# An eight-column scratch result moved into a shared tile, and every later buffer 32 bytes lower

## The chip, the cores and the metric

One Trainium2 chip, one of its cores. The metric is the device time of one execution in microseconds (us): the median of 3 runs of the kernel before is 413.98 us (413.92 to 414.71).

## The reference

A trunk of two decoder layers over 256 tokens of width 1024, all in float32. Layer 0 normalises its input, multiplies it by one wide matrix (z, x, B, C, dt, q, k, v, g side by side), runs a Mamba-2 state-space mixer and a dilated window attention on the results, and multiplies both, side by side, by an output matrix. Layer 1 normalises, multiplies by q, k, v and gate matrices, runs causal attention, gates it, and multiplies by its output matrix. Cut to what matters here:

```
h = rms_norm(x, norm_w)
z, xbc, dt, q, k, v, g = split(h @ even_w_in)
mixed = concat([ssd(xbc, dt) gated by z, dilated_attention(q, k, v) gated by g])
x = x + mixed @ even_w_out
h = rms_norm(x, odd_norm_w)
q, k, v, g = split(h @ odd_w_in)
x = x + (moba_attention(q, k, v) * silu(g)) @ odd_w_out
```

Nearly all the arithmetic is in the products with the four weight matrices.

## The kernel before

**The products.** The weights lie in DRAM cut into tiles of 128 partitions by 2048 columns. `load_split` brings a tile into a buffer `raw` (three buffers, two DMA pieces each) and splits it into a part rounded to float32r, `whi` (a cast on ScalarE), and the rest, `wlo` (a subtraction on VectorE), three buffers of each. Activations are split in the same way: into `xh` and `xl`, one tile each with 8 blocks of 256 tokens, or into pairs of `mix` tiles (24 tiles of 256 columns). A product of float32 numbers is then three TensorE products, high by high, high by low, low by high. There are two forms of it:
- `proj_tok` and `out_proj` (through `mm3`): tokens come out on the partitions. The activations are the stationary operand (128 columns), a row of weights the moving one, 512 columns wide; in the last part of `out_proj`, some are 256 wide. The activations are `mix` tiles in the first three steps and in `out_proj`, and `xh`, `xl` elsewhere.
- `proj_fm`: features come out on the partitions. The weights are the stationary operand, `xh` or `xl` the moving one, 256 columns wide.

In the names of the profile `acc<-whi,xh` is a matmul into the tile acc with whi moving and xh stationary. The smaller products of the mixers and the transposes (`x<-cst,k`, `x<-cst,p` and so on) are plain float32.

**The order.** The program is recorded operation by operation, and the class `Plan` then orders it: it goes through simulated time with a price for every operation, gives an engine the first operation in order of recording that can start, and hands out the buffers of a tag (a set of equal tiles, as the 15 tiles `k2` of 512 columns) by the time of their release, the earliest first. All operations are emitted on one line, L519, in that order.

**The tile of the change.** Line 1252 in `trunk_kernel` issues the first activation of ScalarE, so that the function table is loaded while the first data are still on their way. Its result is never read. It goes to a tile `junk` of 8 columns, which has a tag of its own.

**Where the tiles lie.** Tiles are laid one behind another along the partition when their tag is first used, each rounded up to 32 bytes; the small constants come first. So in the program of the kernel before these start at the following bytes of a partition: xh 16512, xl 24704, cst 32896, all1 39520, k2 42688 (15 tiles of 2048 bytes), junk 73408 (32 bytes), mix 73440 (24 tiles of 1024), raw 98016, whi 122592, wlo 147168 (three tiles of 8192 each), qkT 173472 (four of 4096), p 192288 (18 of 1536), and small ones before, between and behind. xh, xl, cst and k2 start at multiples of 64; mix, raw, whi, wlo, qkT and p at 32 past a multiple of 64, and so does each tile of theirs.

Of the kernel before, what the change touches and what calls it, by code (L numbers as in the profile page):

```python
# [13 lines left out]
AF = mybir.ActivationFunctionType  # L14
# [7 lines left out]
P = 128  # L22
# [538 lines left out]
def trunk_kernel(ctx: ExitStack, tc: tile.TileContext, x, tiles_host, dtw_host, norms, xt_host, params, bparams, consts, causal_mask, out):  # L561
# [5 lines left out]
    pe, act, dve, gps, sp = plan.pe, plan.act, plan.dve, plan.pool, plan.sp  # L567
    count = [0]

    def sb(shape, dt=F32, tag=None, bufs=1, name=None):  # L570
        count[0] += 1
        return plan.tile(shape, tag or f"{name}_{count[0]}", bufs, dt=dt)

    def k2():
        return sb([P, 512], tag="k2", bufs=NK2)
# [53 lines left out]
    nhalf = sb([P, 8], name="nhalf")  # L629
# [619 lines left out]
        pe.matmul(wp[:, 0:128], warm[:, 0:128], warm[:, 0:128], start=True, stop=True)  # L1249
    dve.memset(all1, 1.0)  # L1250

    act.activation(sb([P, 8], name="junk"), nhalf, AF.Copy, scale=1.0)
    sp.dma_start(ncol, norms)
    xf = [two(k2()) for _ in range(4)]
    entry = [tuple(sb([P, S], F32R, tag="mix", bufs=24) for _ in range(2)) for _ in range(KD)]
# [78 lines left out]
    scale = k2()[:, :S]  # L1334
# [80 lines left out]
```

## Time and profile before

| | |
|---|---|
| median of 3 runs | 413.98 us (413.92 to 414.71) |
| the profiled execution | 413.3 us |
| its span, first to last instruction | 411.5 us |
| TensorE busy | 404.1 us |
| VectorE busy | 319.9 us |
| ScalarE busy | 259.5 us |
| read from DRAM | 67.28 MB |

Busy times come from one profiled execution. A busy TensorE is not a TensorE at its peak: consecutive matmuls overlap in the records, so their pace is read from the distance of their starts. The chain of work that ended last is followed back from the last instruction, at each step to what released it. PE is TensorE, PEld its weight loads, DVE VectorE, ACT ScalarE, POOL GpSimd, SP the engine that issues the DMAs.

### The profile page before, as it was taken

The numbers are of one execution on the slowest core, as the hardware profiler recorded it, in microseconds if no ns is written. First come the engines' busy times: TensorE is split into PE (matmuls) and PEld (weight loads), VectorE is DVE, ScalarE is ACT, GpSimd is POOL, SyncE is SP. The second block draws the span as 40 slices with busy tenths as digits, with TensorE's granted clock in tenths as the row PEclk, the third lists the DMA queues.
The fourth block names the chain that finished last, engine by engine and source line by source line (L and its number), as shares of the span: only waits on it lengthen the run. The fifth ranks groups of instructions, "written<-read, shape, count | busy, mean of one in ns | idle before, by whom it ended". The sixth has DMA issues, their size and how long they took to land.

```text
span 411.5 us, 7072 instructions
## 1 busy us (share of the span) xinstructions
PE 404.1 (98%) x2537; PEld 341.7 (83%) x2537; DVE 319.9 (78%) x810; ACT 259.5 (63%) x532; POOL 58.5 (14%) x65
## 2 busy tenths in 40 slices
PE   7999999999999999999999999999999999999996
PEld 6788999999888777778889888878878878879786
DVE  3888899998769999999929774697579856679622
ACT  5887655555346686567775945686559656667610
POOL 0160400000031100242004000013330004500000
PEclk9999999999999999999999999999999999999999
DMA  6995755357454426653645290546650834442003
GB/s 237 377 406 201 249 199 171 103 200 245 166 162 147 147 62 226 224 164 115 220 155 192 64 281 25 143 168 200 206 189 17 255 111 151 166 139 102 2 2 102
DMA packets 23139, 68.84 MB, mean 167 GB/s; under 512 B 4179, under 2 KB 5952, under 8 KB 23104
## 3 DMA queue, kind: packets, MB, share of 16 engines
q1 hardware_dynamic: 23104, 68.39, 49.7%
q8 instruction: 20, 0.33, 0.3%
q14 instruction: 15, 0.12, 0.1%
HBM read 67.28 MB, written 1.10 MB: 166 GB/s over the span
## 4 chain that ended last, share of the span: by engine, by line
PE 91%; DVE 4%; DMA 2%; POOL 1%; issue 1%; ACT 1%; SPq 1%; DVEq 0%
PE acc L519 71%; PE x L519 19%; DMA raw<-in_tiles_dram 2%; DVE wlo L519 1%; DVE k L519 1%; POOL rq L519 1%; DVE xl L519 1%; SPq L519 1%; DVE rq L519 0%; ACT xh L519 0%; ACT whi L519 0%; ACT k L519 0%; DVE t L519 0%; DVEq L519 0%
## 5 line engine op out<-in xcount | busy, mean ns | idle before, releaser
L519 DVE TENSOR_TENSOR wlo<-raw,whi 128x1024 fp32r<-128x1024 f32 (+1 forms) x117 | 140.2, 1212 | 17.5 <-ACT whi L519 17.2
L519 ACT CAST whi<-raw 128x1024 fp32r<-128x1024 f32 (+1 forms) x117 | 119.6, 1043 | 31.7 <-PE acc L519 22.1
L519 PE MATMUL acc<-xh,wlo 128*128 128x256 f32 x288 | 81.2, 282 | 0.0
L519 PE MATMUL acc<-xl,whi 128*128 128x256 f32 x288 | 81.1, 282 | 0.0
L519 PE MATMUL acc<-xh,whi 128*128 128x256 f32 x288 | 80.9, 281 | 0.0
L519 PE MATMUL acc<-whi,xh 128*128 128x512 f32 x192 | 77.8, 406 | 0.0
L519 PE MATMUL acc<-wlo,xh 128*128 128x512 f32 x192 | 77.6, 404 | 0.0
L519 PE MATMUL acc<-whi,xl 128*128 128x512 f32 x192 | 77.4, 403 | 0.0
L519 PE MATMUL acc<-whi,mix 128*128 128x512 f32 x216 | 70.6, 398 | 0.8 <-ACT whi L519 0.8
L519 PEld LDWEIGHTS acc<-xl,whi 128*128 128x128 f32 x288 | 54.3, 188 | 0.4 <-issue 0.2
L519 PEld LDWEIGHTS acc<-xh,whi 128*128 128x128 f32 x288 | 54.3, 189 | 0.2
L519 PEld LDWEIGHTS acc<-xh,wlo 128*128 128x128 f32 x288 | 54.3, 189 | 0.2 <-issue 0.2
L519 PEld LDWEIGHTS acc<-whi,mix 128*128 128x128 f32 x216 | 40.4, 188 | 9.9 <-ACT whi L519 1.8
L519 PEld LDWEIGHTS acc<-whi,xl 128*128 128x128 f32 x192 | 36.4, 189 | 8.9 <-issue 1.2
L519 PE MATMUL acc<-wlo,mix 128*128 128x512 f32 x108 | 43.1, 399 | 0.5 <-DVE wlo L519 0.5
L519 PEld LDWEIGHTS acc<-wlo,xh 128*128 128x128 f32 x192 | 36.4, 190 | 8.5 <-issue 1.4
L519 PEld LDWEIGHTS acc<-whi,xh 128*128 128x128 f32 x192 | 36.4, 189 | 8.1 <-issue 1.0
L519 POOL TENSOR_TENSOR rq<-rq,nhalf 128x8 f32<-128x8 f32 x20 | 36.6, 1831 | 1.5
L519 ACT COPY k<-acc 128x512 f32<-128x512 f32 x24 | 14.1, 586 | 25.3 <-PE acc L519 25.3
L519 PEld LDWEIGHTS acc<-wlo,mix 128*128 128x128 f32 x108 | 20.3, 188 | 5.7 <-DVE wlo L519 1.8
L519 ACT ACTIVATE k<-k 128x512 f32<-128x512 f32 x20 | 12.7, 638 | 18.4 <-DVE k L519 18.4
L519 DVE TENSOR_REDUCE rq<-k 128x8 f32<-128x512 f32 x20 | 13.6, 682 | 12.6 <-ACT k L519 12.6
(151 smaller groups left out, 554.6 us busy)
## 6 DMA issues: line engine op xcount, KB each, us to landing
raw<-in_tiles_dram SPq DMA_DIRECT2D x115, 512.0 KB, 4.8
k<-in_x_dram SPq DMA_DIRECT2D x8, 256.0 KB, 5.6
qkT<-cd SPq DMA_DIRECT2D x4, 512.0 KB, 3.7
k<-in_xt_dram SPq DMA_DIRECT2D x4, 256.0 KB, 6.0
out_dram<-k SPq DMA_DIRECT2D x8, 128.0 KB, 1.8
cst<-in_consts_dram SPq DMA_DIRECT2D x1, 640.0 KB, 9.6
raw<-in_tiles_dram SPq DMA_DIRECT2D x2, 256.0 KB, 4.7
cst<-in_causal_mask_dram SPq DMA_DIRECT2D x1, 192.0 KB, 2.3
```

The costliest lines, as they stand in the source:

```text
L519: getattr(eng[op.engine], op.method)(*[real(a) for a in op.args], **{k: real(v) for k, v in op.kw.items()})
```

## The change

The activation that brings the function table in gets the first 8 columns of a `k2` tile as its output, in place of the tile `junk`.

```diff
-    act.activation(sb([P, 8], name="junk"), nhalf, AF.Copy, scale=1.0)
+    act.activation(k2()[:, :8], nhalf, AF.Copy, scale=1.0)
```

The tag `junk` is gone and with it its 32 bytes. The tags first used after this line (mix, raw, whi, wlo, qkT, p and the small tiles among them) start 32 bytes lower; those first used before it (xh, xl, cst, all1, k2 and others) stay. One `k2` tile more is handed out, after the one that the warm-up uses.

## Rows read from the trace of the kernel before

**Rows 1.** The page: busy time, granted clock, chain that ended last by engine.
```profile
PE 404.1 (98%) x2537; PEld 341.7 (83%) x2537; DVE 319.9 (78%) x810; ACT 259.5 (63%) x532; POOL 58.5 (14%) x65
...
PEclk9999999999999999999999999999999999999999
...
PE 91%; DVE 4%; DMA 2%; POOL 1%; issue 1%; ACT 1%; SPq 1%; DVEq 0%
```

**Rows 2.** The chain in order of time: start us, us, what; five long pieces.
```profile
235 pieces in order of time: start us, us, what
...
18.00 14.12 PE acc L519 x62
...
76.53 27.34 PE acc L519 x233
...
343.43 15.87 PE acc L519 x68
...
397.27 8.19 PE acc L519 x36
...
405.46 2.88 PE x L519 x24
```

**Rows 3.** Groups by shape, PE, 18 to 32 us: busy us, mean ns | idle.
```profile
L519 PE MATMUL acc<-whi,mix 128*128 128x512 f32 x41 | 12.7, 390 | 0.0
...
L519 PE MATMUL acc<-wlo,mix 128*128 128x512 f32 x21 | 8.3, 393 | 0.0
```

**Rows 4.** The same view, 90 to 103 us: one of three alike forms.
```profile
L519 PE MATMUL acc<-xl,whi 128*128 128x256 f32 x38 | 10.6, 280 | 0.0
```

**Rows 5.** The same view, 344 to 358 us: one of three alike forms.
```profile
L519 PE MATMUL acc<-wlo,xh 128*128 128x512 f32 x21 | 8.4, 399 | 0.0
```

**Rows 6.** The same view, 405.5 to 408.3 us.
```profile
L519 PE MATMUL x<-whi,mix 128*128 128x256 f32 x16 | 3.0, 283 | 0.0
```

**Rows 7.** Timeline of ScalarE, 0 to 5 us: start us, us, what, count.
```profile
0.72 1.28 ACT L519 ACT_TABLE_LOAD   x1 [0.72 <-PEq L1386]
2.01 0.21 ACT L519 ACTIVATE junk<-nhalf 128x8 f32<-128x8 f32 x1
3.87 0.91 ACT L519 ACTIVATE mix<-k,ncol 128x256 fp32r<-128x256 f32 x2 [1.65 <-DMA k<-in_xt_dram]
```

**Rows 8.** Groups by shape, whole span: the same work at both places.
```profile
L519 PE MATMUL x<-cst,p 128*128 128x128 f32 x120 | 18.5, 275 | 0.0
...
L519 PE MATMUL x<-cst,k 128*128 128x128 f32 x96 | 14.5, 273 | 1.5 <-DVE k L519 1.5
...
L519 DVE TENSOR_TENSOR xl<-k,xh 128x512 fp32r<-128x512 f32 x4 | 2.7, 684 | 0.0
...
L519 DVE TENSOR_TENSOR wlo<-raw,whi 128x512 fp32r<-128x512 f32 x2 | 1.4, 692 | 2.1 <-ACT whi L519 2.1
...
L519 ACT CAST xh<-k 128x512 fp32r<-128x512 f32 x4 | 2.5, 616 | 0.0
...
L519 ACT CAST whi<-raw 128x512 fp32r<-128x512 f32 x2 | 1.2, 618 | 2.0 <-DMA raw<-in_tiles_dram 2.0
```

**Rows 9.** DMA issues: count, KB each, median us to landing.
```profile
k<-in_xt_dram SPq DMA_DIRECT2D x4, 256.0 KB, 6.0
...
raw<-in_tiles_dram SPq DMA_DIRECT2D x2, 256.0 KB, 4.7
```

**Rows 10.** Groups by shape, whole span: the large matmuls, for their counts.
```profile
L519 PE MATMUL acc<-xh,wlo 128*128 128x256 f32 x288 | 81.2, 282 | 0.0
...
L519 PE MATMUL acc<-whi,xh 128*128 128x512 f32 x192 | 77.8, 406 | 0.0
...
L519 PE MATMUL acc<-whi,mix 128*128 128x512 f32 x216 | 70.6, 398 | 0.8 <-ACT whi L519 0.8
...
L519 PE MATMUL acc<-wlo,mix 128*128 128x512 f32 x108 | 43.1, 399 | 0.5 <-DVE wlo L519 0.5
...
L519 PE MATMUL x<-whi,mix 128*128 128x512 f32 x24 | 7.9, 399 | 0.0
...
L519 PE MATMUL x<-whi,mix 128*128 128x256 f32 x32 | 6.1, 283 | 0.0
```

**Rows 11.** Busy time by stretch: PE, PEld, DVE, ACT, POOL, then clock, DMA share.
```profile
60.00:75.00 15.00, 15.00 (x127) 14.90 (x126) 15.00 (x31) 9.31 (x14) 0.00 (x0) 1.00 0.55 179
135.00:180.00 45.00, 45.00 (x238) 33.36 (x237) 44.53 (x119) 31.83 (x74) 6.74 (x8) 1.00 0.54 173
```

## The prediction

> **What bounds the kernel now.** I read the page first: TensorE is busy for 404.1 of 411.5 us and holds 91% of the chain that ended last [rows 1]. A change is therefore worth what it does to TensorE's pace, or to the few places where TensorE waits. Next I read the chain piece by piece, 235 pieces in all. A long piece of one kind, divided by its number of matmuls, is the distance from one matmul's start to the next; the "mean ns of one" in the group views is no such distance, because matmuls overlap there. The pieces give [rows 2]: 14.12 / 62 = 227.7 ns, 27.34 / 233 = 117.3 ns, 15.87 / 68 = 233.4 ns, 8.19 / 36 = 227.5 ns and 2.88 / 24 = 120.0 ns. What the stretches hold comes from the grouped views of windows inside them. 18 to 32 us is 512 columns wide, weights moving, the stationary operand in mix [rows 3]. 90 to 103 us has 256 columns, xh or xl moving, whi or wlo stationary [rows 4]. 344 to 358 us has 512 columns, weights moving, xh or xl stationary [rows 5]. The tail from 405.5 us has 256 columns, weights moving, mix stationary [rows 6].
>
> At the granted clock, full in nearly the whole span [rows 1], that is 2.4 GHz, 512 columns take 213.3 ns and 256 take 106.7 ns. So each matmul pays an extra 14.3, 20.1, 10.7 or 13.3 ns. The reader should see that 227.7 and 233.4 ns belong to the same operation with the same moving operand; only the place of the stationary tile differs. It is not the stage either: mix has 227.7 ns in the first steps, under full DMA load, and 227.5 ns near the end, where almost nothing else runs.
>
> **Where the bytes lie.** By the placement told above, before the change xh and xl start at a multiple of 64 bytes, and raw, mix, whi, wlo, qkT and p all start 32 bytes past one. After it the latter are at multiples of 64 too. Sorted in this way the rows read:
> - moving at 32, stationary at 32: extra 14.3 (512 columns) and 13.3 ns (256)
> - moving at 32, stationary at 0: extra 20.1 ns (512)
> - moving at 0, stationary at 32: extra 10.7 ns (256)
> - moving at 0, stationary at 0: the trace of before has none; this is what all of them become.
>
> 64 bytes are 16 columns, which is 6.67 ns at this clock. The extras are about 2, 3 and 1.6 such steps. The reading I take: one step always; one more when the moving operand begins in the middle of a 64-byte line and so touches one line more; and up to one more (1 at 512 columns, 0.6 at 256) when the two operands lie at different halves of a line and their reads get in each other's way. By that, both at 0 pay one step: 220.0 ns for 512 columns and 113.3 for 256. This is an estimate extended from four rows to a fifth case.
>
> **The change part by part.** (1) The instruction itself: an 8-column activation of 0.21 us on ScalarE at 2.01 us; ScalarE's next instruction starts only at 3.87 us, when a load has landed [rows 7]. It writes eight columns to another address: 0 us, covered by that wait of 1.65 us. (2) The free tile is one of the 15 k2 tiles. The planner hands tiles out by the earliest release, and this one is back before any other; only five tiles (the warm-up's and four loads) are taken before the first product's results, so no step has to wait for it and the planned order stays. The tile that inherits its place is written by ScalarE itself, which is in order: 0 us. Queues, DMAs and counts of instructions are otherwise the same.
>
> (3) 32 bytes for ScalarE and VectorE. The trace has the same operation at both places: a 512-column cast takes 618 ns from raw to whi (at 32) and 616 ns from k to xh (at 0); the 512-column subtraction takes 692 against 684 ns [rows 8]. For the 117 casts and subtractions this bounds the effect at 0 to -1 us of VectorE's busy time, off the path. TensorE's fp32 transposes from k (at 0) and p (at 32) have means of 273 and 275 ns [rows 8]; these I leave at 0.
>
> (4) DMA. A 256 KB transfer lands in 4.7 us in raw (at 32) and in 6.0 us in k (at 0) [rows 9]; nothing shows raw to be the slower, and DMA is 2% of the chain [rows 1]. I take 0, with bounds of -0.3 and +0.3 us for the start, where the chain hangs on loads.
>
> (5) TensorE's products, the one term that counts. The counts [rows 10]: 192 for each of three forms with xh or xl stationary, 576 in all; 216 + 108 + 24 with mix stationary and 512 columns, and half of 24 again for wlo, 360; 32 and half of it again, 48, with 256 columns; 288 for each of three forms with xh or xl moving, 864. So:
> - 576 x (233.4 - 220.0) = 7.7 us
> - 360 x (227.6 - 220.0) = 2.7 us
> - 48 x (120.0 - 113.3) = 0.3 us
> - 864 x (117.3 - 113.3) = 3.5 us
>
> Sum 14.2 us, if TensorE stays the bound everywhere. It does not quite. In 60 to 75 us VectorE is busy for all 15 us and in 135 to 180 us for 44.53 of 45 [rows 11], so there a faster TensorE waits for VectorE next. These 60 us are 15% of TensorE's time: 2.1 us of the sum less the 0.5 us that VectorE has free, 1.6 us lost. Most of the 235 pieces of the chain are short, with small products or waits between the large matmuls [rows 2]; as an allowance for these I take off a tenth of the remaining 12.6 us, 1.3 us. That leaves about 11 us. The span goes from 411.5 to 400.5 us; the profiled execution took 413.3 us, that is 1.8 us around the span, and comes to 402.3 us; the median of 413.98 is 0.7 above it, so I predict 403.0 us.
>
> The missing case is bounded from both sides by the nearest rows: no better than one step (the lowest extra, 10.7 ns, is between one and two), and no worse than the 20.1 ns of the only rows with a stationary tile at 0.
>
> **Rivals.** *Only part of it goes.* If the two effects hang on larger blocks than 64 bytes (xh begins at a multiple of 128, whi after the change does not), one of them stays. Taking away only the split line gives 936 x 6.67 + 48 x 6.67 = 6.6 us; taking away only the conflict gives 576 x 5.8 = 3.3 us, and 864 matmuls that end between 113.3 and 120.0, from -3.5 to +2.3 us. These give 407 to 413 us.
>
> *Slower: a stationary tile at a multiple of 64 is itself the bad case.* The one clean comparison in the trace, 233.4 against 227.6 ns, can be read so: +5.8 ns for every load of a tile at 0. Then the 864 matmuls with whi or wlo stationary, and the 408 with mix, all get it: 1272 x 5.8 = 7.4 us, all on the path, since a slower TensorE needs no cover; a moving operand at 0 may give back 936 x 2.7 = 2.5 us (120.0 against 117.3). About 419 to 421 us. It decides as soon as the stretch with mix stationary rises above 229 ns. For it: it needs no second effect. Against it: a tile at 0 fills fewer lines than one at 32.
>
> *No change.* xh and xl lie low in the memory, from byte 16512 to 32896, and mix far above, so the 5.8 ns can belong to the region, which 32 bytes don't alter; or the buffers do not move. Then 414.0 us. [...]
>
> **How the numbers follow.** Forecast as summed, 400 to 405 us: 0.40. Part of it, 405 to 413.1: 0.22. No change, 414.0 within 0.2%: 0.20. Slower by the rival, around 420: 0.18. A difference of 0.2%, 0.8 us, is about what measurements of this kernel can tell from none. Faster is therefore 0.62, same 0.20, slower 0.18. The range from 400.0 to 415.0 us takes in the first three and leaves the last out.
>
> **What would show it.** In the trace after: the long pieces of the chain at about 220 ns (512 columns, whether mix or xh is stationary), the 256-column stretch at about 113 ns, and VectorE nearer to full between 135 and 180 us of the old time. If xh falls to 227 and mix stays, the conflict alone is gone; if both fall by 6.7 and keep their distance, the split line alone. If mix rises to 233, the slower rival is right. If all four distances stay within 1 ns, addresses of this kind do not matter here, and the forecast is wrong at its root. If the distances fall as told and the time falls by under 7 us, the cover by VectorE was underestimated.

## The result, and the profile after

| | before | after |
|---|---|---|
| median | 413.95 us (413.54 to 414.71, 4 runs) | 409.01 us (408.95 to 409.77, 4 runs) |
| the profiled execution | 413.3 us | 408.95 us |
| its span | 411.5 us | 407.1 us |
| TensorE busy | 404.1 us | 399.1 us |

The ratio is 0.9883, with a 95% interval of 0.9864 to 0.9901: faster by 4.9 us or 1.2%. Faster was forecast, and 409.01 us lies in the range. But 11 us had been told, and the forecast as summed was 400 to 405 us: the range holds the time only because it takes in two of the rivals.

The page after, its lines of busy time and of the chain's engines, answers to [rows 1]:

```profile
PE 399.1 (98%) x2537; PEld 338.1 (83%) x2537; DVE 319.6 (78%) x810; ACT 259.5 (64%) x532; POOL 59.6 (15%) x65
...
PE 90%; DVE 4%; DMA 2%; POOL 1%; issue 1%; ACT 1%; SPq 1%; DVEq 0%
```

TensorE has 5.0 us less of products and 3.6 us less of weight loads. VectorE and ScalarE stayed within 0.3 us; GpSimd, 1% of the chain, has 1.1 us more. The chain in order of time (start us, us, what) shows where; these are the pieces of [rows 2]:

```profile
18.48 14.13 PE acc L519 x62
...
76.43 26.43 PE acc L519 x233
...
339.90 15.59 PE acc L519 x68
...
392.92 8.19 PE acc L519 x36
...
401.11 2.88 PE x L519 x24
```

The long pieces are the same, in the same order, so nothing here speaks for another planned order. By the counts: with mix stationary 14.13 / 62 = 227.9 ns and 8.19 / 36 = 227.5 ns, where 227.7 and 227.5 had been; in the tail 2.88 / 24 = 120.0 ns, as before. With xh stationary 15.59 / 68 = 229.3 ns, where 233.4 had been. With xh moving 26.43 / 233 = 113.4 ns, where 117.3 had been. The starts add it up: 0.5 us later than before at the first piece, 0.1 us earlier at the second, 3.5 us earlier at the third, 4.4 us earlier at the fourth.

The time from each start to the next, put down to the first of the two and summed over the whole trace, went from 105.8 to 102.6 us for the products with xh or xl moving, from 141.5 to 139.9 us for those with xh or xl stationary, and stayed at 88.1 and 5.6 us for those with mix. Unrounded that is 3.2 and 1.5, together 4.7 us; the small products took 0.3 us more, and so it accounts for the span's 4.4 us.

### The profile page after: what moved, and what is told of

Its sections match the earlier page's. It is cut to its first block, busy times and chain, and to the rows that moved or that the text cites. A ratio compares the mean times of both kernels' runs of the same rounds, so it can differ in the third digit from the quotient of the medians.

```text
span 407.1 us, 7072 instructions
## 1 busy us (share of the span) xinstructions
PE 399.1 (98%) x2537; PEld 338.1 (83%) x2537; DVE 319.6 (78%) x810; ACT 259.5 (64%) x532; POOL 59.6 (15%) x65
## 4 chain that ended last, share of the span: by engine, by line
PE 90%; DVE 4%; DMA 2%; POOL 1%; issue 1%; ACT 1%; SPq 1%; DVEq 0%
PE acc L519 71%; PE x L519 20%; DMA raw<-in_tiles_dram 2%; DVE wlo L519 1%; DVE k L519 1%; POOL rq L519 1%; DVE xl L519 1%; SPq L519 1%; DVE rq L519 0%; ACT xh L519 0%; ACT whi L519 0%; ACT k L519 0%; DVE t L519 0%; DVEq L519 0%
## 5 line engine op out<-in xcount | busy, mean ns | idle before, releaser
L519 PE MATMUL acc<-xh,wlo 128*128 128x256 f32 x288 | 80.2, 278 | 0.0
L519 PE MATMUL acc<-xl,whi 128*128 128x256 f32 x288 | 80.0, 278 | 0.0
L519 PE MATMUL acc<-xh,whi 128*128 128x256 f32 x288 | 79.9, 277 | 0.0
```

The costliest lines, as they stand in the source:

```text
L519: getattr(eng[op.engine], op.method)(*[real(a) for a in op.args], **{k: real(v) for k, v in op.kw.items()})
```

## The experiments

In what follows the distance is the moving operand's first byte less the stationary one's, modulo 256 (that 256 is the right number comes out of the map below). The time from one matmul's start to the next is called the pace. By the placement of the kernel before, weights start at 224 and xh at 128 modulo 256. So where xh is stationary the distance was 96, and where it moves 160. After the change (weights at 192) they are 64 and 192. Between weights and mix it is 0 both times.

**Is it the place, or the shared tile?** Two kernels separate them. The first keeps the shared tile and puts the 32 bytes back, as an edit of the changed kernel:

```diff
     act.activation(k2()[:, :8], nhalf, AF.Copy, scale=1.0)
+    pool.tile([P, 8], F32, name="pad")
```

> The changed kernel with an unused 32-byte tile behind the k2 tiles: the shared tile stays in use, all addresses are those of before. If the places of the buffers are the whole cause: the time of before, 413.9 us, with 117.3 and 233.4 ns in the two stretches. If the use of the shared tile (another order of buffers) is the cause: 409.0 us.

Measured: 413.89 us, 0.9994 of the kernel before (0.9979 to 1.0009). The second keeps the tile of its own, as an edit of the kernel before:

```diff
-    act.activation(sb([P, 8], name="junk"), nhalf, AF.Copy, scale=1.0)
+    act.activation(sb([P, 128], name="junk")[:, :8], nhalf, AF.Copy, scale=1.0)
```

> The kernel before with its own junk tile made 512 bytes long in place of 32: later buffers lie 480 bytes higher, which is the same place modulo 512 as in the changed kernel. If places modulo 512 (or a smaller power of two) are the cause: 409.0 us. If the absolute place or the shared tile is: 413.9 us.

Measured: 408.55 us, 0.9872 (0.9846 to 0.9899). The same pieces of the two chains, first with the padding, then with the long tile of its own (start us, us, what):

```profile
77.18 27.34 PE acc L519 x233
...
344.05 15.87 PE acc L519 x68
```

```profile
76.33 26.43 PE acc L519 x233
...
339.74 15.59 PE acc L519 x68
```

27.34 and 15.87 us are the numbers of before, 26.43 and 15.59 those of after. The shared tile does nothing, the places are the whole cause, and 480 bytes up does what 32 bytes down does: the place counts modulo 512 or less.

**Whose place?** Mix alone moved, an edit of the changed kernel:

```diff
+    pool.tile([P, 8], F32, name="pad")
     load_xf(0)
```

> The changed kernel with an unused 32-byte tile between mix and raw: mix at the place of after, raw, whi, wlo and all later buffers at the place of before. Distance theory: the stretches with xh go back to 233.4 and 117.3 ns (+4.7 us), and those with mix leave 227.6 ns, since mix and weights are now 32 bytes apart; if that costs up to 6 ns, 360 x 6 = up to 2.2 us more: 413.7 to 416 us. Own-place theory: mix keeps 227.6 ns or goes to 233 ns, as xh does with the same weights. Nothing but xh and weights matters: 413.7 us.

Measured: 415.44 us, 1.0045 (1.0030 to 1.0061), slower than the kernel before, and in the 413.7 to 416 us of the distance theory. Its chain:

```profile
18.59 14.50 PE acc L519 x62
...
77.74 27.34 PE acc L519 x233
...
345.23 15.87 PE acc L519 x68
...
399.19 8.40 PE acc L519 x36
```

xh is back at 117.3 and 233.4 ns, and mix went from 227.7 to 14.50 / 62 = 233.9 and 8.40 / 36 = 233.3 ns. The weights lie here as in the kernel before, mix as in the changed one; both of those have 227.6 ns. What makes the pace is thus not the place of either operand but how the two lie to each other.

**The map.** To measure that by itself, a kernel runs series of 24 matmuls back to back, each series on a line of its own, both operands in one tile `z` at chosen offsets (here s and m, in steps of 8 bytes). For 256 columns the blocks of the moving operand are 256 wide in place of 512 (shortened):

```
st = lambda k, lo: z[:, LO * lo + 256 * k + 2 * s:][:, :P]
mv = lambda k, lo: z[:, B0 + LO * lo + 512 * (k % 4) + 2 * m:][:, :512]
for k in range(8):
    out += [(st(k, 0), mv(k, 0)), (st(k, 0), mv(k, 1)), (st(k, 1), mv(k, 0))]
```

> Leaves the trunk out: TensorE alone, 86 series of 24 matmuls of the kernel's two forms on constant data, all operands in one tile, each series with the stationary and the moving operand at stated byte offsets (modulo 512) in steps of 32 bytes. Distance theory (only the distance between the two operands' places, modulo some power of two, sets the pace): a series with both moved alike keeps the pace of offset 0, near 227.6 ns (512 columns) and 120 ns (256); a distance of 64 bytes gives 229.3 and 113.4 ns, one of 96 bytes 233.4 and 117.3 ns, the same whichever operand is moved. Line theory (the forecast's): both at multiples of 64 gives 220 and 113.3 ns, both at 32 past one 227 and 120. Own-place theory: the pace follows the offset of one operand whatever the other's. Region theory: a stationary operand 80 KB further on at the same offset modulo 512 changes the pace by 4 ns or more, and offsets do little.

Measured, from its chain. L50: 512 columns, the stationary operand moved by 256 bytes; L58, L59, L60 and L67: the moving one by 32, 64, 96 and 320; L73 and L74: both by 32, both by 64; L81: nothing moved, the stationary tile 80 KB further on. L87: 256 columns, the stationary operand moved by 64, so that the distance is 192. L102, L106 and L110: 256 columns, the moving operand at 64, 192 and 320; L117: both at 64.

```profile
57.50 5.45 PE acc L50 x24
...
102.05 5.60 PE acc L58 x24
107.66 5.50 PE acc L59 x24
113.16 5.61 PE acc L60 x24
...
152.26 5.50 PE acc L67 x24
...
185.79 5.45 PE acc L73 x24
191.24 5.47 PE acc L74 x24
...
229.54 5.45 PE acc L81 x24
...
257.47 2.83 PE acc L87 x24
...
300.04 2.72 PE acc L102 x24
...
311.30 2.73 PE acc L106 x24
...
322.57 2.83 PE acc L110 x24
...
342.38 2.86 PE acc L117 x24
```

A distance of 0 has 5.45 / 24 = 227 ns wherever the two lie (at most, the first series of all aside, 5.49 / 24 = 229, both moved by 192), 32 and 96 have 233, 64 has 229, and 320 is as 64. Over the last 16 starts of each series, in ns:

| distance | 0 | 32 | 64 | 96 | 128 | 160 | 192 | 224 |
|---|---|---|---|---|---|---|---|---|
| 512 columns | 226.7 | 233.4 | 228.9 | 233.6 | 233.4 | 234.1 | 233.3 | 233.3 |
| 256 columns | 120.0 | 116.7 to 117.9 | 113.3 or 117.8 | 120.1 | 118.9 | 117.4 | 113.3 or 117.8 | 118.4 |

Two numbers stand where series of one distance settled differently. For 512 columns the distance theory holds to within 1 ns, the first series of all aside (228.4 ns at 0), and the line, own-place and region theories fall. For 256 columns it holds to within 1.2 ns at six of the eight distances. At 64 and 192 the pace is not the same whichever operand is moved, as had been expected: at 192 the two series with the moving operand moved have 113.3 and 113.4 ns and the two with the stationary one moved 117.8 (L106 and L87 above); at 64 one of four has 113.3. There something besides the distance has a say. The table has the kernel's own numbers to within 1 ns: 233.4 and 117.3 ns at 96 and 160, 229.3 and 113.4 ns at 64 and 192, 227.6 and 120.0 ns at 0.

**Does the table foretell the kernel?** Two other places for all later buffers, as edits of the changed kernel, first at distance 0, then at 128:

```diff
     act.activation(k2()[:, :8], nhalf, AF.Copy, scale=1.0)
+    pool.tile([P, 48], F32, name="pad")
```

```diff
     act.activation(k2()[:, :8], nhalf, AF.Copy, scale=1.0)
+    pool.tile([P, 16], F32, name="pad")
```

> The changed kernel with an unused 192-byte tile behind the k2 tiles: weights and xh at distance 0 modulo 256 everywhere, mix and weights too. Distance theory with the map's numbers: 226.7 ns where xh is stationary (half of the gain as yet not taken there), 120.0 ns where xh moves. Against the kernel before: -510 x 6.5 = -3.3 us and +866 x 2.0 = +1.7 us, so about 412.1 us; slower than the changed kernel by 3 us. Line theory: nothing changes against the changed kernel, 409 us.

> The changed kernel with an unused 64-byte tile behind the k2 tiles: later buffers start at multiples of 256, xh at 128 past one. Distance theory: 233.4 ns where xh is stationary, 118.9 ns where it moves: against the kernel before 0 and +866 x 1.0 = +0.9 us, about 414.6 us. Line theory: all buffers at multiples of 64 as in the changed kernel, so 409 us.

Measured: dist_0 412.66 us, 0.9981 (0.9969 to 0.9994), against 412.1 expected; dist_128 413.34 us, 0.9993 (0.9984 to 1.0003), against 414.6. Their chains, in that order:

```profile
78.62 27.94 PE acc L519 x233
...
288.85 15.45 PE acc L519 x68
```

```profile
76.55 27.66 PE acc L519 x233
...
343.40 15.87 PE acc L519 x68
```

At distance 0: 27.94 / 233 = 119.9 and 15.45 / 68 = 227.2 ns. At 128: 118.7 and 233.4 ns. All four are the table's to within 1 ns. The time of dist_128 is 1.3 us under what was worked out from them; the paces are foretold better than the time. In dist_128 every large buffer lies at a multiple of 64, as in the changed kernel, and the gain is gone: multiples of 64 are not what counts.

**What kind of cost is it?** The same bench with finer distances, with only the low or the high tiles moved, and with other formats (`t=y` is bf16, `t=g` plain float32):

```diff
-        def pairs(n, s, m, a=0):
+        def pairs(n, s=(0, 0), m=(0, 0), t=None, count=24):
```

> Leaves the trunk out: TensorE alone, 58 series on constant data. (a) Distances of 4 to 112 bytes: if lines of 32 bytes or more matter, distances of 4 to 16 bytes keep the 226.7 and 120.0 ns of distance 0; if the exact phase of the two streams matters, they leave them at once. (b) Only the low or only the high stationary tile moved by 96 bytes: if a matmul is slowed by the weights that are loaded while it streams (those of the next one), a series with every third load at a distance has a mean between 226.7 and 233.6 ns, and it is the second of each three that grows; if its own stationary place matters, it is the third. (c) bf16 operands (half the bytes per column) and plain float32 (more passes per column): if the cost comes from two streams that together come near what the memory delivers, neither changes with the distance by more than 1 ns per matmul (bf16 near 216 ns at 512 columns); if it comes from a start-up step of every matmul, they change as the first form does.

Measured, the series of its chain: L48 and L49 are 512 columns at distances of 4 and 8 bytes, L85 and L87 bf16 at 32 and 96, L100 and L103 plain float32 at 0 and 96 (two matmul records for each product):

```profile
13.59 5.70 PE acc L48 x24
19.29 5.61 PE acc L49 x24
...
164.04 5.18 PE acc L85 x24
...
174.40 5.18 PE acc L87 x24
...
221.26 6.87 PE acc L100 x16
...
241.86 6.87 PE acc L103 x16
```

(a) 4 bytes are enough to leave the 226.7 ns of the map: over the last 12 starts 237.7 ns at 4, 233.3 at 8, 231.7 at 16; with 256 columns, 123.3 ns at 4. So the exact distance counts, not lines of 8 bytes or more. (c) bf16 has 215.8 ns at all eight distances, 109.2 with 256 columns, and plain float32 429.2 ns per record at all six. Of the three formats tried only float32r, whose columns of four bytes take 226.7 ns at best where bf16's of two take 215.8 (512 columns), feels the distance. That is what had been expected of two streams (the moving columns, and the weights of the next matmul, whose load starts within 10 ns of the running matmul's start in the timeline of the changed kernel from 340.5 to 341.5 us). No run shows the memory itself, so why the distance counts is not shown. (b) was to tell whose weights matter, and did not: with one load in three moved by 96 bytes (a distance of 160) the mean is 232.1 ns, inside the bounds, but all three places of the pattern move.

**Can both forms be had at their best?** The table has 226.7 ns at 0 and 113.3 at 64, and a weight tile is used in one form only. So its place in the buffer can depend on the form. (What the expectation calls a distance of 64, the stationary weights 64 bytes further on, is 192 as counted here; the table has the same two paces for both.)

```diff
+    pool.tile([P, 48], F32, name="pad")
...
-        hi = sb([P, nk, n], F32R, tag="whi", bufs=NW)
-        lo = sb([P, nk, n], F32R, tag="wlo", bufs=NW)
+        off = 16 if nk == 8 else 0
+        hi, lo = (sb([P, 2112], F32R, tag=t, bufs=NW)[:, off:off + 2048].rearrange("p (a b) -> p a b", a=nk)
+                  for t in ("whi", "wlo"))
```

> The changed kernel with an unused 192-byte tile behind the k2 tiles, and the buffers whi and wlo 256 bytes longer: a weight tile that will be the moving operand goes to the buffer's start (distance 0 to xh and mix), one that will be stationary goes 64 bytes further (distance 64). Distance theory: 226.7 ns with xh stationary (230.3 in the changed kernel), 113.3 to 114.2 ns with xh moving: 510 x 3.3 = 1.7 us below the changed kernel, about 407.3 us. If something else is the next bound: 409 us.

Measured: 408.82 us, 0.9888 (0.9866 to 0.9909), no better than the changed kernel. Two like stretches of its chain, 100 matmuls each with xh moving for nearly all:

```profile
308.07 12.43 PE acc L519 x100
...
363.72 12.01 PE acc L519 x100
```

With xh stationary it has the 15.45 us of dist_0, as hoped. But where xh moves, one stretch runs at 113.3 ns and the other at 117.8 through all its matmuls, at one and the same distance; in the changed kernel, also at 192, both took 12.05 us:

```profile
308.45 12.05 PE acc L519 x100
...
363.92 12.05 PE acc L519 x100
```

So the two paces of the table are two states, 113.3 and 117.8 ns, and each of these two stretches stays in one. Over the kernel the mean is 115.3 ns in place of 114.2, which eats what the other form gained. What sets the state? The bench again, each series behind a number of small matmuls:

```diff
+            for _ in range(5): nc.tensor.matmul(wp[:, :128], f[:, :128], f[:, :128], start=True, stop=True)
             for go, end, w, v in pairs(256, m=(16, 16), count=48): nc.tensor.matmul(accs[2][:, :256], w, v, start=go, stop=end)
```

> Leaves the trunk out: TensorE alone on constant data. The 256-column form at sixteen distances (0 to 240 bytes in steps of 16), four series of 48 each, every series behind 1, 3, 5 or 7 small float32 matmuls; then the 512-column form at distances 0 and 64. If a series settles into one of several paces by the moment at which it starts, the four series of one distance differ by 4 ns (113.3 and 117.8 ns at 64 and 192, as the map showed and as two_places has more often than the changed kernel); if the distance alone sets it, they agree within 0.5 ns. A distance whose four series all have 113.3 ns would be the better place; 512 columns at distance 0 should have 226.7 ns in all four.

Measured: the four series at 64, 112 and 192 all settle at 113.3 ns (L81, L105, L145 below), those at 16 at anything from 113.3 to 118.8 (L61, L63).

```profile
53.30 5.45 PE acc L61 x48
...
60.31 5.70 PE acc L63 x48
...
118.50 5.45 PE acc L81 x48
...
196.91 5.50 PE acc L105 x48
...
327.60 5.46 PE acc L145 x48
```

512 columns have 226.7 to 227.4 ns at 0 and 228.8 at 64, in four series each. So this run has no second state at 64 or 192, though the map has it at both and two_places at 192; the number of small matmuls ahead does not bring it out. Two edits of two_places with the stationary weights at other places, and the changed kernel, unedited, beside them:

```diff
-        off = 16 if nk == 8 else 0
+        off = 48 if nk == 8 else 0
```

```diff
-        off = 16 if nk == 8 else 0
+        off = 36 if nk == 8 else 0
```

> As two_places, but a weight tile that will be stationary goes 192 bytes behind the buffer's start, so that xh lies 64 bytes past it modulo 256 in place of 192. If the distance alone sets the pace: 113.3 to 114 ns with xh moving, 228.6 ns with xh stationary, and 866 x 1.2 = 1.0 us below two_places, about 407.8 us. If the pace hangs on the moment at which a stretch starts: 113 to 118 ns mixed as in two_places, about 408.8 us.

> As two_places, but the stationary weight tiles 144 bytes behind the buffer's start, a distance of 112 bytes, which had 113.3 ns in five series of five. If this distance has one settled pace: 113.3 to 114 ns with xh moving, about 407.8 us. If not: 408.8 us or more.

> The changed kernel as it is, on the same chip as the other two: 409.0 us, 0.988 of the kernel before.

Measured: 409.42 us, 0.9902 (0.9887 to 0.9916); 412.68 us, 0.9980 (0.9971 to 0.9990); 408.93 us, 0.9888 (0.9872 to 0.9905). At 64 the two states are mixed again, mean 115.7 ns. At 112, which had 113.3 ns in every series tried, the kernel has another state:

```profile
76.77 27.96 PE acc L519 x233
```

27.96 / 233 = 120.0 ns. What selects the state is open. One difference was not isolated by any run: in these three kernels a weight buffer is 8448 bytes long, so neighbouring buffers differ by 256 modulo 512, while in the changed kernel and on the bench all weights of a series lie alike modulo 512. No version tried beats the changed kernel by more than its interval.

## Why the prediction was right and wrong, point by point

- *The bound.* Right. TensorE held 91% of the chain and its pace gave the whole gain; the starts of the long pieces show it arriving piece by piece.
- *The instruction and the free tile, 0 us.* Right: pad_back, with the shared tile, has the time of before, and own_512, without it, that of after.
- *ScalarE and VectorE, 0 us.* Right: 259.5 us both times, and 319.9 against 319.6 us.
- *DMA, 0 with 0.3 us either way.* Nothing shows an effect of place. But the first long piece starts between 17.8 and 19.7 us over the runs, whatever the places; it was 18.00 before and 18.48 after. The bound was too narrow for one execution.
- *The products: the step that failed.* The missing case, both operands at a multiple of 64, was given one step of 6.67 ns, 220.0 and 113.3 ns. The 2.4 GHz behind the step, and the 213.3 and 106.7 ns for the columns alone, stand in no row of before; the bench has 215.8 less 109.2, 106.6 ns for 256 columns of bf16, that is 2.40 columns a ns. The line of 64 bytes was the author's reading, and no run shows one. Measured: mix and weights, both at multiples of 64, kept two steps (227.9, 227.5 and 120.0 ns). With xh stationary the pace fell to 229.3 ns only; the 113.3 came with xh moving alone (113.4). So a moving operand that begins 32 bytes past a multiple of 64 costs nothing by that (226.7 ns with both operands there and with both at 64, in the map), and the sorting of the four rows by 32 and 0 was a wrong reading of right rows. What those rows held in common was a distance of 0, 96 or 160 modulo 256. "At different halves" came near it, but in the map the distance counts modulo 256 (512 columns at 256 have the 227 ns of 0, at 320 the 229 of 64), and the change leaves the two 64 apart, not together.
- *The terms.* 864 with xh moving: forecast 3.5 us, measured 3.2. This term was right by luck: 192 happens to be one of the two distances of the map that can have 113.3 ns, which has nothing to do with multiples of 64 (118.7 ns in dist_128), and the changed kernel got that pace where two_places got 117.8 ns for a part. 576 with xh stationary: 7.7 against 1.5 us; 64 takes off 4.1 ns in the undisturbed stretch and not 13.4, and less elsewhere. 360 with mix: 2.7 against 0. 48 in the tail: 0.3 against 0. The sum is 4.7 where 14.2 stood.
- *The cover by VectorE and the allowance, 1.6 and 1.3 us taken off.* Of the 4.7 us only 0.3 are missing in the span. The gain that was real came through: in 60 to 75 us and in the 45 us that answer to 135 to 180 [rows 11] VectorE is as full as before, and TensorE is still busy throughout (below). The forecast of 11 us was thus not too large for want of cover; what was taken off hid a part of the error of the sum. Whether 14.2 us would have been covered, no run shows.

```profile
60.00:75.00 15.00, 15.00 (x131) 14.90 (x130) 15.00 (x32) 9.26 (x14) 0.00 (x0) 1.00 0.56 189
133.00:178.00 45.00, 45.00 (x241) 33.65 (x240) 44.77 (x119) 32.12 (x74) 6.70 (x8) 1.00 0.54 175
```

- *The rivals.* "Only part of it goes" has the time, 407 to 413 us, and half of the reason: the effects hang on more than the place within 64 bytes (with every large buffer at a multiple of 64 both times, xh moving has 113.4 ns after the change and 118.7 in dist_128). Of the signs told, its "xh falls to 227 and mix stays" came nearest: xh fell to 229.3 and mix stayed. The slower rival was refuted where it said it would be: the stretch with mix stayed at 227.5 to 227.9 ns, under 229. "No change" was refuted by the result, and the region by the map (226.7 ns with the stationary tile 80 KB further on). That the pace hangs on addresses held for float32r alone: with 512 columns the distance moves it from 226.7 to as much as 237.7 ns, while bf16 has 215.8 ns and plain float32 429.2 ns per record at every distance tried.

The rows themselves could have warned: they had mix and weights at distance 0 with two steps, and the change leaves that distance as it is. A reading by distances would have kept mix at 227.6 ns and thereby taken 3.0 us off the sum at once.

## What to carry to other kernels

Where float32r matmuls bound a kernel, the first bytes of the stationary and the moving operand modulo 256 belong to its tuning: read the distance between starts for each pair of tiles, and lay the buffers so that the form with the most time has its good distance (here 0 for 512 columns, 226.7 against up to 234.1 ns, 3% of a matmul, with buffers 32 bytes apart; 64 or 192 for 256, against 120.0 ns at 0 worth 6% where the stretch settles at 113.3 ns and 2% where it settles at 117.8, which only a trace tells). For bf16 and plain float32 the runs show nothing to gain (215.8 and 429.2 ns at every distance tried). Any tile ahead of such buffers whose size is not a multiple of 256 bytes, even an unused one, can shift them and change the time (pad_back: an unused one of 32 bytes, 413.89 us in place of 409.01); in comparisons of other edits, hold the placement fixed. When a pattern of four known cases is extended to a fifth, ask what the known cases have in common besides the label they were sorted by, and which quantity the change leaves alone.

## What the runs showed of the hardware that was not expected

- On the bench, at a granted clock of 1.0, a float32r matmul starts 226.7 to 237.7 ns after the one before it with 512 columns and 113.3 to 123.3 ns with 256, by the distance of its operands modulo 256, down to 4 bytes. bf16 has 215.8 and 109.2 ns at all eight distances; by an estimate from the difference of these two, 106.6 ns for 256 columns, the columns alone take about 213 and 107 ns, so that bf16 pays some 2.5 ns beside them and float32r 7 to 24.
- At one distance, 192, a stretch of two_places settled at 113.3 ns and a like one at 117.8, and each kept its pace for its whole length of 100 matmuls; at a distance of 112 it was 113.3 ns in all five series tried and 120.0 in the kernel. What selects the pace is open.
